# Column means of an 8192 x 8192 matrix: the mid-stream loads move to GpSimd's queue, eight descriptors to a packet

## The chip, the cores and the metric

The kernel runs on one core of a Trainium2 chip. A core has five engines with an instruction stream each: TensorE (PE, matmuls), VectorE (DVE, elementwise work on 128 partitions), ScalarE (ACT), GpSimd (POOL) and SyncE (SP, which here only issues transfers and waits). Data comes from the device's memory into the on-chip memory SBUF through 16 DMA engines, which work through queues of descriptors. A descriptor names one contiguous piece to be moved. TensorE writes its sums to a memory of its own, PSUM.

The metric is the device time of one execution in microseconds (us). The profile gives the span of one profiled execution, which is a little shorter than the time.

## The reference

```python
def setup_inputs():
    return {"x": np.random.randn(8192, 8192).astype(np.float32)}

def reference(x):
    return np.mean(x, axis=0)
```

The input has 268.4 MB, the output 32 KB. Each element is read once and added once. What is computed is a sum over 8192 rows for each of 8192 columns, divided by 8192.

## The kernel before

The 8192 rows are 64 groups of 128 rows, one row for each partition. VectorE adds group after group into an accumulator `acc` of 128 x 8192. Then TensorE sums over the 128 partitions: a matmul with a matrix `ones` whose elements are 1/8192. The last groups go to TensorE without passing VectorE.

SBUF holds six row buffers of 32 KB per partition each. Four of them, in two pairs, receive loads; the fifth (`both`) takes the sum of a pair; the sixth is `acc`.

```python
bufs = sb.tile([P, U, N], f32, name="bufs")      # P = 128, U = 6, N = 8192
both = bufs[:, U - 2, :]
acc = bufs[:, U - 1, :]
...
def load(dst, src):                              # every load comes from SyncE
    ins = tc.keep_in_program_order(nc.sync.dma_start(out=dst, in_=src)).ins
    ...
def load_rows(g, u, n):                          # n row groups; a partition gets n adjacent rows
    return load(bufs[:, u:u + n, :], rows(g, n).rearrange("(p j) c -> p j c", j=n))
```

With n = 2 each partition gets two adjacent rows, 64 KB that are contiguous in the device's memory and in SBUF.

The stream begins with part of a late row group (`head`), four row groups at once, two row groups, and part of the last row group (`ahead`):

```python
headed = load(head[:], rows(G - 4)[:, :3 * F])                # 768 KB, F = 512, G = 64
first, second = load_rows(0, 0, 4), load_rows(4, 4, 2)        # 16 MB, 8 MB
early = load(ahead[:], rows(G - 1)[:, 8 * F:WHOLE * F])       # 1 MB, WHOLE = 12
add(bufs[:, 2:4, :], bufs[:, 2:4, :], bufs[:, 0:2, :], [first])
add(bufs[:, 4:6, :], bufs[:, 4:6, :], bufs[:, 2:4, :], [second])
add(acc, acc, both, [])
```

Mid-stream has 24 rounds. Each loads two row groups and adds them:

```python
while g < G - 10:                                 # g = 6, 8, ..., 52
    u = (g + 2) % 4
    dma = load_rows(g, u, 2)
    add(both, bufs[:, u, :], bufs[:, u + 1, :], [dma])   # frees the pair of buffers
    add(acc, acc, both, [])
    if g == 20:
        add(acc[:, 8 * F:WHOLE * F], acc[:, 8 * F:WHOLE * F], ahead[:], [early])
    if g == 28:
        add(acc[:, :3 * F], acc[:, :3 * F], head[:], [headed])
    g += 2
```

`add` is a VectorE addition. Where it needs a transfer and the add ahead of it, a no-op on ScalarE (or now and then GpSimd) waits for both and releases the addition.

The end: six single row groups, two cut ones, group 62 (loaded whole) and group 63 in pieces. The last piece, columns 7168 to 8191, is loaded as two blocks of 512 columns, and each block is summed by four matmuls of 128 columns, so that the first block can be summed while the second is still on its way.

```python
for lo, hi in [(0, 8), (12, 14), (14, 15), (15, 16)]:
    load(r63[:, lo * F:hi * F], rows(g)[:, lo * F:hi * F])
plan = [(acc, 3, 5), (acc, 0, 3), (r61, 0, 5), (acc, 5, 12), (r62, 0, 12), (r62, 12, 13),
        (acc, 12, 14), (acc, 14, 16), (r63, 0, 8), (r63, 12, 14), (r63, 14, 15), (r63, 15, 16)]
```

`plan` is the order of the matmuls on TensorE; numbers are blocks of 512 columns. ScalarE and VectorE then copy the sums from PSUM to SBUF, and four small stores write the result.

Of the kernel before, what the change touches and what calls it, by code (L numbers as in the profile page):

```python
# [9 lines left out]
def kernel(  # L10
# [27 lines left out]
    nc = tc.nc  # L38
    f32 = mybir.dt.float32
    M, N = x.shape  # L40
    P = nc.NUM_PARTITIONS
    F = 512
    W = F // 2
    WHOLE = 12
    G = M // P
# [3 lines left out]
    sb = ctx.enter_context(tc.tile_pool(name="sb", bufs=1))  # L49
    psp = ctx.enter_context(tc.tile_pool(name="psum", bufs=1, space=bass.MemoryType.PSUM))  # L50

    bufs = sb.tile([P, U, N], f32, name="bufs")
    both = bufs[:, U - 2, :]
    acc = bufs[:, U - 1, :]
    ones = sb.tile([P, 32], f32, name="ones")
    ahead = sb.tile([P, 4 * F], f32, name="ahead")
    tail = sb.tile([P, 2, F // 4], f32, name="tail")
    warm = sb.tile([P, 32], f32, name="warm")
    nc.gpsimd.memset(ones[:], 1.0 / M)  # L59
    ready = sb.tile([P, 1], f32, name="ready")  # L60
    tc.keep_in_program_order(
        nc.gpsimd.tensor_add(out=ready[:], in0=ones[:, 0:1], in1=ones[:, 1:2]))  # L62
    banks = [psp.tile([P, F], f32, name=f"bank{b}") for b in range(3)]
    ends = [psp.tile([P, W], f32, name="end0"), psp.tile([P, 2, F // 4], f32, name="end1")]

    loads = []

    def landed(*inss):

        nop = tc.keep_in_program_order(nc.sync.nop()).ins  # L70
        for o in inss:
            tc.add_manual_dep(nop, o.name, sync, reason="SyncE waits")

    def load(dst, src):
        ins = tc.keep_in_program_order(nc.sync.dma_start(out=dst, in_=src)).ins
        k = len(loads)
        over = loads[k - 8:k - 6] if k >= 8 and k % 2 == 0 else []
        tc.declare_no_dep(ins, group="loads", keep=over, reason="the reader of the buffer waited")
        for o in over:
            tc.add_manual_dep(ins, o.name, sync, reason="covers the next load too")  # L80
        tc.add_to_no_dep_group("loads", ins)
        loads.append(ins)
        return ins

    def rows(g, n=1):
        return x[g * P:(g + n) * P, :]

    def load_rows(g, u, n):
        return load(bufs[:, u:u + n, :], rows(g, n).rearrange("(p j) c -> p j c", j=n))

    adds, joins = [], {}

    def add(dst, a, b, dmas):

        ins = nc.vector.tensor_add(out=dst, in0=a, in1=b).ins  # L95
        if dmas and adds:
            waiter = nc.scalar if len(adds) % 8 > 1 else nc.gpsimd
            nop = joins[waiter] = tc.keep_in_program_order(waiter.nop()).ins  # L98
            for o in dmas + adds[-1:]:
                tc.add_manual_dep(nop, o.name, sync, reason="the no-op waits")  # L100
            for group in ("loads", "adds"):
                tc.declare_no_dep(ins, group=group, reason="the no-op waited")
            tc.add_manual_dep(ins, nop.name, sync, reason="waits for both at once")
        elif adds:
            tc.declare_no_dep(ins, group="loads", reason="the add ahead waited")
        tc.add_to_no_dep_group("adds", ins)
        adds.append(ins)

    head = sb.tile([P, 3 * F], f32, name="head")
    headed = load(head[:], rows(G - 4)[:, :3 * F])  # L110
    first, second = load_rows(0, 0, 4), load_rows(4, 4, 2)
    early = load(ahead[:], rows(G - 1)[:, 8 * F:WHOLE * F])
    add(bufs[:, 2:4, :], bufs[:, 2:4, :], bufs[:, 0:2, :], [first])
    add(bufs[:, 4:6, :], bufs[:, 4:6, :], bufs[:, 2:4, :], [second])
    add(acc, acc, both, [])
    tc.keep_in_program_order(nc.scalar.copy(out=warm[:], in_=ones[:]))  # L116
    g = 6
    while g < G - 10:
        u = (g + 2) % 4
        dma = load_rows(g, u, 2)  # L120
        add(both, bufs[:, u, :], bufs[:, u + 1, :], [dma])
        add(acc, acc, both, [])
        if g == 20:
            add(acc[:, 8 * F:WHOLE * F], acc[:, 8 * F:WHOLE * F], ahead[:], [early])
        if g == 28:
            add(acc[:, :3 * F], acc[:, :3 * F], head[:], [headed])
        g += 2

    while g < G - 4:
        row = bufs[:, (g + 2) % 4, :]  # L130
        add(acc, acc, row, [load(row, rows(g))])
        g += 1
    for lo, loaded in [(3, 3), (5, 0)]:
        row = bufs[:, (g + 2) % 4, :]
        dma = load(row[:, loaded * F:], rows(g)[:, loaded * F:])
        add(acc[:, lo * F:], acc[:, lo * F:], row[:, lo * F:], [dma])
        g += 1
    r61, r62, r63 = [bufs[:, (g + 1 + j) % 4, :] for j in range(3)]
    load(r62, rows(g))
    tc.keep_in_program_order(nc.gpsimd.tensor_add(  # L140
        out=acc[:, 13 * F:], in0=acc[:, 13 * F:], in1=r62[:, 13 * F:]))
    g += 1
    for lo, hi in [(0, 8), (12, 14), (14, 15), (15, 16)]:
        load(r63[:, lo * F:hi * F], rows(g)[:, lo * F:hi * F])

    plan = [
        (acc, 3, 5),
        (acc, 0, 3),
        (r61, 0, 5),
        (acc, 5, 12),  # L150
        (r62, 0, 12),
        (r62, 12, 13),
# [1 line left out]
        (acc, 14, 16),  # L154
        (r63, 0, 8),
        (r63, 12, 14),
        (r63, 14, 15),
        (r63, 15, 16),
    ]
    sums = []  # L160
    for row, lo, hi in plan:
        if lo < WHOLE:
            for i in range(lo, hi):
                sums.append((banks[i // 4], i % 4, banks[i // 4], row[:, i * F:(i + 1) * F]))
        elif lo < 14:
            for c in range(lo * F, hi * F, W):
                e, q = divmod(c // W - 2 * WHOLE, 4)
                sums.append((ends[e], q, ends[e], row[:, c:c + W]))
        else:
            cols = row[:, 14 * F:].rearrange("p (b q c) -> p b q c", b=2, q=4)  # L170
            for q in range(4):
                b = slice(lo - 14, hi - 14)
                sums.append((ends[1], q, ends[1][:, b, :], cols[:, b, q, :]))
    for n, (dst, q, part, cols) in enumerate(sums):
        tc.keep_in_program_order(nc.tensor.matmul(  # L175
            out=part[32 * q:32 * q + 32],
            lhsT=ones[:],
            rhs=cols,
            start=all(d is not dst or k != q for d, k, _, _ in sums[:n]),
            stop=all(d is not dst or k != q for d, k, _, _ in sums[n + 1:]),  # L180
            tile_position=(0, 32 * q),
            skip_group_check=True,
        ))

    res = both[:, :3 * F].rearrange("p (b c) -> p b c", b=3)
    first_end = both[:, 3 * F:3 * F + W]

    def copy(dst, src):
        tc.keep_in_program_order(nc.scalar.copy(out=dst, in_=src))  # L189

    def store(engine, dst, src, *then):
        ins = tc.keep_in_program_order(engine.dma_start(out=dst, in_=src)).ins
        for o in then:
            tc.add_manual_dep(ins, o.name, sync, reason="follows that load")
        return ins

    copy(res[:, 2, :], banks[2][:])
    s2 = store(nc.scalar, out[8 * F:12 * F].rearrange("(q c) -> q c", q=4), res[0:P:32, 2, :],
               loads[-4])
    for b in range(2):  # L200
        copy(res[:, b, :], banks[b][:])
    copy(first_end, ends[0][:])
    nc.vector.tensor_copy(out=tail[:], in_=ends[1][:])  # L203
    landed(*loads[-8:-6])
    landed(*loads[-6:-4])
    landed(loads[-4])
    landed(*joins.values())
    s01 = store(nc.sync, out[:8 * F].rearrange("(b q c) -> q b c", b=2, q=4), res[0:P:32, 0:2, :])
    s3 = store(nc.scalar, out[12 * F:14 * F].rearrange("(q c) -> q c", q=4), first_end[0:P:32, :])
    store(nc.sync, out[14 * F:].rearrange("(b q c) -> q b c", b=2, q=4), tail[0:P:32, :, :])  # L210
    landed(loads[-3], s2)
    landed(loads[-2])
    landed(loads[-1], adds[-1])
    landed(s01, s3)
    hold = tc.keep_in_program_order(nc.vector.nop()).ins
# [31 lines left out]
```

## Time and profile before

| what | value |
|---|---|
| time, median of 3 | 629.1 us (629.0 to 629.31) |
| span of the profiled execution | 627.2 us |
| VectorE busy | 530.1 us (85%) |
| TensorE busy | 15.4 us (2%) |
| ScalarE, GpSimd busy | 3.5 us, 4.0 us |
| one addition of 128 x 8192 on VectorE | 8.69 us, 55 of them |
| one issue of a load on SyncE (median) | 0.33 us |
| one 8 MB load, issue to landing (median of its kind) | 29.9 us |

The page of the profile has parts: busy time by engine; the span in 40 equal slices, each with a digit for the busy share in tenths; the DMA queues with packets, bytes and the time that packets took; the chain of work that ended last, followed back from the end; groups of instructions with their mean duration and the idle time before them. A line such as `L95 DVE TENSOR_TENSOR` means line 95 of the kernel, VectorE, an addition of two tensors. `POOLq` and `ACTq` are instructions of these engines' queues that don't count as work, such as the no-ops. An engine's idle time costs something only if that engine is what the end waits for.

### The profile page before, as it was taken

Reading aid. Unit: us, or ns where it says so; the run is one execution under the profiler, and the core shown is the slowest. Engines: PE = TensorE matmul, PEld = TensorE weight load, DVE = VectorE, ACT = ScalarE, POOL = GpSimd, SP = SyncE. Lnnn points to the kernel's source line nnn. Section 1 sums busy time; section 2 is a strip of 40 time slices with the busy share of each in tenths; the row PEclk is TensorE's granted clock in tenths of the full one; section 3 lists DMA queues with packets and bytes.
Section 4 is the critical chain, followed back from the end, with each engine's and each line's share of the span. In section 5 each row is a group of like instructions: output and inputs, shape, how many; then the busy total and the mean of one; then the engine's idle time right before and its main releaser. Section 6 shows DMA issues by size and latency. Waiting matters only on the chain.

```text
span 627.2 us, 468 instructions
## 1 busy us (share of the span) xinstructions
PE 15.4 (2%) x118; PEld 4.9 (1%) x118; DVE 530.1 (85%) x62; ACT 3.5 (1%) x6; POOL 4.0 (1%) x7
## 2 busy tenths in 40 slices
PE   0000000000000000000000000000000000000027
PEld 0000000000000000000000000000000000000002
DVE  0028999999888999988998889888898888999991
ACT  0000000000000000000000000000000000000001
POOL 0000000000000000000000000000000000000002
PEclk9999999999999999999999999999999999999999
DMA  9999999999999999999999999999999999999996
GB/s 385 468 401 415 455 468 401 460 410 451 418 447 422 426 443 422 447 410 460 405 464 401 468 401 468 401 468 401 468 402 464 405 464 403 428 430 430 433 435 273
DMA packets 6074, 268.50 MB, mean 428 GB/s; under 512 B 672, under 2 KB 684, under 8 KB 1208
## 3 DMA queue, kind: packets, MB, share of 16 engines
q1 hardware_dynamic: 6056, 268.46, 99.1%
q8 instruction: 1, 0.02, 0.0%
q10 hardware_dynamic: 16, 0.01, 0.0%
q14 instruction: 1, 0.01, 0.0%
HBM read 268.44 MB, written 0.03 MB: 428 GB/s over the span
## 4 chain that ended last, share of the span: by engine, by line
DMA 55%; DVE 33%; another core or an unknown queue 10%; PE 0%; issue 0%; ACTq 0%; POOL 0%; POOLq 0%
DMA bufs<-in_x_dram 55%; DVE bufs L95 33%; PE bank L175 0%; PE end L175 0%; ACTq L98 0%; DVE tail L203 0%; POOLq L98 0%; POOL ready L62 0%; POOL ones L59 0%; POOLq L231 0%
## 5 line engine op out<-in xcount | busy, mean ns | idle before, releaser
L95 DVE TENSOR_TENSOR bufs<-bufs 128x8192 f32<-128x8192 f32 (+3 forms) x59 | 525.6, 8909 | 84.3 <-DMA bufs<-in_x_dram 43.7
L175 PE MATMUL bank<-bufs,ones 128*32 128x512 f32 x74 | 12.7, 713 | 608.7 <-DVE bufs L95 608.2
L203 DVE COPY tail<-end 128x256 f32<-128x256 f32 x1 | 0.4, 424 | 10.1 <-PE end L175 10.1
L175 PEld LDWEIGHTS bank<-bufs,ones 128*32 128x32 f32 x74 | 3.1, 120 | 616.9 <-issue 616.2
L140 POOL TENSOR_TENSOR bufs<-bufs 128x1536 f32<-128x1536 f32 x1 | 3.5, 3463 | 615.3 <-DMA bufs<-in_x_dram 615.3
L189 ACT COPY bufs<-bank 128x512 f32<-128x512 f32 x3 | 1.8, 585 | 619.8 <-PE bank L175 617.2
L175 PE MATMUL end<-bufs,ones 128*32 128x256 f32 (+1 forms) x44 | 3.2, 345 | 0.0
L95 DVE TENSOR_TENSOR bufs<-bufs,ahead 128x2048 f32<-128x2048 f32 x1 | 2.3, 2291 | 0.1
L95 DVE TENSOR_TENSOR bufs<-bufs,head 128x1536 f32<-128x1536 f32 x1 | 1.8, 1759 | 0.1
L175 PEld LDWEIGHTS end<-bufs,ones 128*32 128x32 f32 x44 | 1.8, 109 | 2.1 <-issue 0.8
L116 ACT ACT_TABLE_LOAD x1 | 1.3, 1283 | 0.7 <-PEq L231 0.7
L189 ACT COPY bufs<-end 128x256 f32<-128x256 f32 x1 | 0.4, 378 | 0.0
L116 ACT COPY warm<-ones 128x32 f32<-128x32 f32 x1 | 0.2, 218 | 0.0
L62 POOL TENSOR_TENSOR ready<-ones 128x1 f32<-128x1 f32 x1 | 0.2, 193 | 0.1
L59 POOL MEMSET ones<- 128x32 f32 x1 | 0.1, 124 | 0.3 <-POOLq L231 0.3
L231 POOL MEMSET const-bfloat16-1.0<- 128x1 bf16 x1 | 0.1, 101 | 0.0
L231 POOL MEMSET const-uint8-127<- 128x1 uint8 x1 | 0.1, 101 | 0.0
L231 POOL MEMSET const-float32-0.0<- 128x1 f32 x1 | 0.1, 98 | 0.2 <-issue 0.2
L231 POOL MEMSET const-float32-1.0<- 128x1 f32 x1 | 0.1, 98 | 0.0
## 6 DMA issues: line engine op xcount, KB each, us to landing
bufs<-in_x_dram SPq DMA_DIRECT2D x8, 4096.0 KB, 26.4
bufs<-in_x_dram SPq DMA_DIRECT2D x1, 3328.0 KB
bufs<-in_x_dram SPq DMA_DIRECT2D x1, 2048.0 KB, 20.3
ahead<-in_x_dram SPq DMA_DIRECT2D x1, 1024.0 KB
head<-in_x_dram SPq DMA_DIRECT2D x1, 768.0 KB
bufs<-in_x_dram SPq DMA_DIRECT2D x1, 512.0 KB, 21.1
bufs<-in_x_dram SPq DMA_DIRECT2D x2, 256.0 KB, 21.4
bufs<-in_x_dram SPq DMA_DIRECT2D x26, 29.9
```

Of the source, the lines that this page charges most:

```text
L59: nc.gpsimd.memset(ones[:], 1.0 / M)
L62: nc.gpsimd.tensor_add(out=ready[:], in0=ones[:, 0:1], in1=ones[:, 1:2]))
L95: ins = nc.vector.tensor_add(out=dst, in0=a, in1=b).ins
L116: tc.keep_in_program_order(nc.scalar.copy(out=warm[:], in_=ones[:]))
L140: tc.keep_in_program_order(nc.gpsimd.tensor_add(out=acc[:, 13 * F:], in0=acc[:, 13 * F:], in1=r62[:, 13 * F:]))
L175: tc.keep_in_program_order(nc.tensor.matmul(out=part[32 * q:32 * q + 32], lhsT=ones[:], rhs=cols, start=all(d is not dst or k != q for d, ...
L189: tc.keep_in_program_order(nc.scalar.copy(out=dst, in_=src))
L203: nc.vector.tensor_copy(out=tail[:], in_=ends[1][:])
L231: nc = _bacc.Bacc("TRN2", target_bir_lowering=False, num_devices=1)
```

## The change

The 24 mid-stream loads are issued by GpSimd in place of SyncE, with `single_packet=True`. In such a load each of the 16 DMA engines moves eight descriptors of 64 KB, and these form one packet. It is for a smaller cost of packets in the long middle of the stream.

Around it other parts differ. The no-ops all run on ScalarE, since GpSimd's stream now stands at its own loads. `ahead` and `head` are no longer added by VectorE in mid-stream; TensorE sums them at the end. The last piece of group 63 is one load of 1024 columns, summed by four matmuls of 256 columns.

```diff
+    def load_soft(dst, src):
+        ins = tc.keep_in_program_order(
+            nc.gpsimd.dma_start(out=dst, in_=src, single_packet=True)).ins
+        k = len(soft)
+        over = soft[k - 8:k - 7] if k >= 8 else []
+        ...
+        return ins
...
-            waiter = nc.scalar if len(adds) % 8 > 1 else nc.gpsimd
+            waiter = nc.scalar
...
-        dma = load_rows(g, u, 2)
+        dma = load_rows(g, u, 2, load_soft)
         add(both, bufs[:, u, :], bufs[:, u + 1, :], [dma])
         add(acc, acc, both, [])
-        if g == 20:
-            add(acc[:, 8 * F:WHOLE * F], acc[:, 8 * F:WHOLE * F], ahead[:], [early])
-        if g == 28:
-            add(acc[:, :3 * F], acc[:, :3 * F], head[:], [headed])
...
-    for lo, hi in [(0, 8), (12, 14), (14, 15), (15, 16)]:
+    for lo, hi in [(0, 8), (12, 14), (14, 16)]:
         load(r63[:, lo * F:hi * F], rows(g)[:, lo * F:hi * F])
...
     plan = [
+        (ahead, 8, 12),
         (acc, 3, 5),
         (acc, 0, 3),
         (r61, 0, 5),
+        (head, 0, 3),
         (acc, 5, 12),
...
-        (r63, 14, 15),
-        (r63, 15, 16),
+        (r63, 14, 16),
```

The rest of the diff (cut) follows from this: PSUM tiles and stores of the last piece have the plain order of columns, and the waits before the end name one load fewer.

More of the change, by code (lines that the diff above doesn't have):

```diff
@@ L56 @@
     ahead = sb.tile([P, 4 * F], f32, name="ahead")
-    tail = sb.tile([P, 2, F // 4], f32, name="tail")
+    tail = sb.tile([P, W], f32, name="tail")
     warm = sb.tile([P, 32], f32, name="warm")
@@ L63 @@
     banks = [psp.tile([P, F], f32, name=f"bank{b}") for b in range(3)]
-    ends = [psp.tile([P, W], f32, name="end0"), psp.tile([P, 2, F // 4], f32, name="end1")]
+    ends = [psp.tile([P, W], f32, name=f"end{e}") for e in range(2)]
     loads = []
@@ L72, in landed @@
             tc.add_manual_dep(nop, o.name, sync, reason="SyncE waits")
+    soft = []
+    def load_soft(dst, src):
[3 more added lines that the diff above has]
+        over = soft[k - 8:k - 7] if k >= 8 else []
+        tc.declare_no_dep(ins, group="loads", keep=over, reason="the reader of the buffer waited")
+        tc.add_to_no_dep_group("loads", ins)
+        soft.append(ins)
+        return ins
     def load(dst, src):
@@ L86, in rows, with load_rows @@
         return x[g * P:(g + n) * P, :]
-    def load_rows(g, u, n):
-        return load(bufs[:, u:u + n, :], rows(g, n).rearrange("(p j) c -> p j c", j=n))
+    def load_rows(g, u, n, how=load):
+        return how(bufs[:, u:u + n, :], rows(g, n).rearrange("(p j) c -> p j c", j=n))
     adds, joins = [], {}
@@ L109 @@
     head = sb.tile([P, 3 * F], f32, name="head")
-    headed = load(head[:], rows(G - 4)[:, :3 * F])
+    load(head[:], rows(G - 4)[:, :3 * F])
     first, second = load_rows(0, 0, 4), load_rows(4, 4, 2)
-    early = load(ahead[:], rows(G - 1)[:, 8 * F:WHOLE * F])
+    load(ahead[:], rows(G - 1)[:, 8 * F:WHOLE * F])
     add(bufs[:, 2:4, :], bufs[:, 2:4, :], bufs[:, 0:2, :], [first])
@@ L161 @@
     for row, lo, hi in plan:
+        base = 8 * F if row is ahead else 0
         if lo < WHOLE:
             for i in range(lo, hi):
-                sums.append((banks[i // 4], i % 4, banks[i // 4], row[:, i * F:(i + 1) * F]))
-        elif lo < 14:
+                cols = row[:, i * F - base:(i + 1) * F - base]
+                sums.append((banks[i // 4], i % 4, cols))
+        else:
             for c in range(lo * F, hi * F, W):
                 e, q = divmod(c // W - 2 * WHOLE, 4)
[L168 to L174, printed above, removed]
+                sums.append((ends[e], q, row[:, c:c + W]))
+    for n, (dst, q, cols) in enumerate(sums):
         tc.keep_in_program_order(nc.tensor.matmul(
-            out=part[32 * q:32 * q + 32],
+            out=dst[32 * q:32 * q + 32, :],
             lhsT=ones[:],
             rhs=cols,
-            start=all(d is not dst or k != q for d, k, _, _ in sums[:n]),
-            stop=all(d is not dst or k != q for d, k, _, _ in sums[n + 1:]),
+            start=all(d is not dst or k != q for d, k, _ in sums[:n]),
+            stop=all(d is not dst or k != q for d, k, _ in sums[n + 1:]),
             tile_position=(0, 32 * q),
@@ L185 @@
     res = both[:, :3 * F].rearrange("p (b c) -> p b c", b=3)
-    first_end = both[:, 3 * F:3 * F + W]
+    tails = [both[:, 3 * F:3 * F + W], tail[:]]
     def copy(dst, src):
@@ L195, in store, with end @@
         return ins
+    def end(e):
+        return (out[(WHOLE + 2 * e) * F:(WHOLE + 2 * e + 2) * F].rearrange("(q c) -> q c", q=4),
+                tails[e][0:P:32, :])
     copy(res[:, 2, :], banks[2][:])
     s2 = store(nc.scalar, out[8 * F:12 * F].rearrange("(q c) -> q c", q=4), res[0:P:32, 2, :],
-               loads[-4])
+               loads[-3])
     for b in range(2):
         copy(res[:, b, :], banks[b][:])
-    copy(first_end, ends[0][:])
-    nc.vector.tensor_copy(out=tail[:], in_=ends[1][:])
+    copy(tails[0], ends[0][:])
+    nc.vector.tensor_copy(out=tails[1], in_=ends[1][:])
     landed(*loads[-8:-6])
     landed(*loads[-6:-4])
-    landed(loads[-4])
+    landed(*loads[-4:-2])
     landed(*joins.values())
     s01 = store(nc.sync, out[:8 * F].rearrange("(b q c) -> q b c", b=2, q=4), res[0:P:32, 0:2, :])
[L209 to L212, printed above, removed]
+    s3 = store(nc.scalar, *end(0))
+    store(nc.sync, *end(1))
+    landed(loads[-2], s2)
     landed(loads[-1], adds[-1])
```

## The prediction

> **What bounds the kernel now.** I read the page first, then the chain of waits in order of time, then who waits for whom, and the groups by shape for the end. From the page, the rows of the 40 slices, the queue and the traffic:
>
> ```profile
> DVE  0028999999888999988998889888898888999991
> DMA  9999999999999999999999999999999999999996
> ...
> q1 hardware_dynamic: 6056, 268.46, 99.1%
> ...
> HBM read 268.44 MB, written 0.03 MB: 428 GB/s over the span
> ```
>
> The DMA row has a 9 in every slice but the last: the 16 DMA engines are busy from start to end, while VectorE is at 8 or 9 and has holes. All loads lie on one queue, 6056 packets, and their packets took 99.1% of 16 engines' span. 0.991 x 627.2 = 621.6 us, so only 5.6 us of the span are not transfer (about 2 us before the first packet, about 3.5 us after the last). The neighbouring slices that alternate between 401 and 468 GB/s are packets booked to one slice or the next; I read means of long stretches alone.
>
> The chain of waits (start, length, what), a piece of mid-stream:
>
> ```profile
> 190.35 29.93 DMA bufs<-in_x_dram
> 220.28 0.04 POOLq L98
> 220.31 0.02 issue
> 220.34 8.70 DVE bufs L95
> 229.04 0.02 issue
> 229.06 29.92 DMA bufs<-in_x_dram
> ```
>
> A load is issued when the first add of a pair frees its buffers, and lands 29.93 us later. From 190.35 to 229.06 are 38.71 us, and in this time two loads of 8 MiB pass (two pairs of buffers, so the chain hops over every second load): 16.78 MB / 38.71 us = 433.4 GB/s, 19.36 us a load. So of the 29.93 us, 29.93 - 19.36 = 10.6 us are queueing behind the load before. This is the margin by which an issue may be late in mid-stream before a DMA engine runs dry.
>
> At the start the margin is smaller:
>
> ```profile
> 63.10 17.24 DVE bufs L95
> 80.33 0.02 issue
> 80.36 8.70 DVE bufs L95
> 89.06 0.02 issue
> 89.08 0.05 ACTq L98
> 89.13 0.02 issue
> 89.15 8.70 DVE bufs L95
> 97.85 0.02 issue
> ```
>
> The second load of the program has landed at 63.0. Behind it lies the 1 MiB of "ahead" (1.05 MB / 433.4 = 2.4 us), to 65.4. The first of the 24 mid-stream loads is issued at 60.95 (the timeline shows SyncE issuing there): 4.4 us of margin. It ends at 65.4 + 19.36 = 84.8; the second is issued at 80.33: again 4.4. The third is issued at 97.85, when the one before it ends at 104.1: 6.3. VectorE then catches up and the margin grows to 10.6.
>
> The end, from the waits in total and the groups by shape:
>
> ```profile
> DVE bufs L95 <- ACTq L98: 25.2, 13, 2.6
> DVE bufs L95 <- POOLq L98: 13.2, 7, 2.2
> ...
> L175 PE MATMUL end<-bufs,ones 128*32 128x256 f32 x28 | 2.7, 382 | 0.0
> L175 PE MATMUL end<-bufs,ones 128*32 128x128 f32 x16 | 0.8, 279 | 0.0
> ```
>
> The no-ops named there only hand on a landing: VectorE waits 25.2 + 13.2 = 38.4 us in 20 places for loads. It isn't the bound. What remains is how fast the DMA engines go through their packets, and the few us after the last landing (PE's last matmuls, one copy of 0.42 us, one store).
>
> **What the Trainium skill says.** (1) "DMA: Bandwidth & Descriptors", section "Where 436 GB/s comes from": 16 ports x 32 B x 850 MHz = 435.2 GB/s is the ceiling, 27.2 GB/s an engine. The trace agrees from below: 433.4 in mid-stream. So at most 0.4% is to be had while bytes stay the same. (2) The same page, "Why small descriptors are slow (HBM only)": a fixed overhead of some 3 cycles for each packet inside the engine, which joining descriptors in one packet spreads out; it holds this worthwhile only up to 256 B. The trace shows a constant per descriptor of that kind: its single records of 64 KiB last 2421 ns on average and those of 32 KiB 1217 ns, and twice 1217 less 2421 is 13 ns. By the pace of mid-stream it is 19.36 us / 8 = 2419 ns a descriptor against 65536 B / 27.2 = 2409 ns: 10 ns. How much of this belongs to the packet rather than to the descriptor, no run here shows. (3) The same page, "Queues, rings and completion order": an engine goes round robin between its queues, a whole packet at a time. The kernel before has a single load queue, so its trace is silent. (4) "SBUF — State Buffer", section "Who interferes with whom": a VectorE instruction with two SBUF inputs contends with GpSimd's reads of SBUF only, and GpSimd's writing of descriptors is inferred to go on beside it. Before, GpSimd issues no load, so the trace is silent here too.
>
> **The change part by part.**
>
> 1. *24 loads as one packet of eight.* There are 24 x 8 = 192 descriptors of 64 KiB per engine in these loads, 24 x 19.36 = 464.6 us of the stream. If the whole 10 ns belongs to the packet, seven of eight are saved: 24 x 7 x 10 ns = 1.7 us. If only 3 cycles do, at the 850 MHz of the ceiling, it is 24 x 7 x 3.5 ns = 0.6 us. I take the middle: -1.2 us. As every load's add waits for its landing and the stream never pauses, each ns saved per load moves all that follows, so this counts in full.
>
> 2. *GpSimd issues in place of SyncE.* SyncE's issue takes 0.33 us by the trace; what one by GpSimd takes no run here shows. Up to 4.4 us (the smallest margin; then 6.3, and up to 10.6) it is hidden. I choose to believe that it is: 0.
>
> 3. *Two queues at the seams.* At the first seam the 8 MiB packet group arrives after 60.95, when the second load has about one descriptor per engine left (its last starts 2.4 us before 63.0) and the 1 MiB of "ahead" waits behind. "ahead" may now come later by one soft packet, 19 us; nothing needs it before the end, since its add is gone from VectorE. At the second seam the row loads from SyncE arrive while the last packet group runs, and with one packet per engine they can't cut in: 0.
>
> 4. *VectorE loses two adds* (2.29 + 1.76 = 4.05 us). They lay in mid-stream, where it waits 1.9 us a load: 0. All no-ops move to ScalarE, the same 0.03 to 0.05 us each: 0.
>
> 5. *PE gains seven matmuls.* Four on "ahead" run early. Three on "head" come between the row-61 matmuls and the wait for the last add, while PE is still slow: 34 records take 7.95 us there, 0.23 each, so 6 records 1.4 us. PE then starts the last acc columns at about 615, and row 62 up to 0.5 us later than now. The GpSimd add that ends at 619.86 gates PE anyway, so I count 0 to 0.1 us.
>
> 6. *Last piece whole.* One load of 512 KB, eight descriptors of 4 KiB per engine, in place of sixteen of 2 KiB: -8 x 10 ns = -0.08 us. After its landing PE has four matmuls of 256 columns (eight records, mean 382 ns, overlapped) in place of four of 128 (279 ns): +0.1 to 0.2. Together with part 5: +0.1 us.
>
> Sum: 629.1 - 1.2 + 0.1 = 628.0 us.
>
> **The rivals.**
>
> *The constant belongs to the descriptor, not to the packet.* Then part 1 gives nothing, and 629.1 + 0.1 = 629.2 results. For it: tiny records of 4 B in the trace also last 9 ns, so a descriptor costs something in whatever packet. Against: the wording of the skill. I give it a third.
>
> *Descriptors can't be written while VectorE adds.* An add starts 0.02 us after every issue, and lasts 8.7. The second mid-stream load would then be late by 8.7 - 4.4 = 4.3 us, the third a little more, and later ones stay within 10.6. The engines would show holes near 85 and 105 us, and the time would be 633 to 636. Against: the skill's inference. I give it 6%.
>
> *The soft ring is slower.* Its descriptors must be fetched from somewhere; 10 ns more per descriptor cost 192 x 10 ns = 1.9 us: 631. A first issue that takes over 4.4 us would add a hole of a few us once. 12%.
>
> *A big packet cuts ahead at the first seam.* If the first packet group starts on an engine before the second load's last descriptors, that load lands up to 19 us late, VectorE is late for all that follows, and the time goes towards 640. For: nothing orders two queues. Against: at 60.95 all but about one descriptor per engine are done. 2%.
>
> **Range and chances.** The best case is the ceiling for the 24 loads, 629.1 - 1.9 - 0.2 = 627.0; the common bad case is the slower ring or a late first issue, 630.5. These hold about eight in ten: 626.9 to 630.5. Faster by over 2% would be under 616.5 us, where 268.44 MB / 435.2 alone are 616.8: 1% for what I don't understand. Slower by over 2% is over 641.7 us, which only the cutting packet or holes in every load reach: 3%.
>
> **What would show it.** In the profile after: a second queue with 201 MB; the step between two landings at 19.27 to 19.30 us in place of 19.36 (part 1 right), or 19.36 (constant per descriptor), or more (slower ring); 9s in the DMA row from 60 to 110 us (no holes, parts 2 and 3); VectorE's second add of the double buffers still starting at 63.1; VectorE busy 526 us; PE's last matmuls ending within 0.2 us of where they stand against the last landing. The prediction is wrong if issues by GpSimd take over 4 us, or if the two queues share the engines in a way that delays a landing on which an add waits.

## The result, and the profile after

The changed kernel takes 631.44 us (631.28 to 631.52), the kernel before 629.05 us beside it. The ratio is 1.0037, with a 95% interval of 1.002 to 1.0054: the change costs 2.4 us. It was predicted to gain 1.1, and the range ended at 630.5.

The page of the changed kernel: 40 slices, queues and traffic.

```profile
DVE  0028999998888998888988889888889886999992
...
DMA  9999999999999999999999999999999999999995
...
q0 software_dynamic: 3456, 201.33, 73.9%
q1 hardware_dynamic: 2452, 67.13, 24.8%
...
HBM read 268.44 MB, written 0.03 MB: 426 GB/s over the span
```

The DMA row has no hole. The two queues' packets took 73.9% + 24.8% of 629.6 us, 621.4 us, where the one queue took 621.6 us before: nothing was saved, and nothing was lost either. What is new stands in VectorE's row: a 6 in slice 34 (about 519 to 535 us) where all its neighbours have 8 or 9.

The chain of waits of the changed kernel shows the pace of mid-stream, and then what became of the end. Columns are start, length, what.

```profile
191.20 0.52 POOL bufs L78
191.73 18.80 issue
...
210.54 0.52 POOL bufs L78
...
500.82 33.31 DMA bufs<-in_x_dram
534.12 0.03 ACTq L110
534.16 0.02 issue
534.18 8.70 DVE bufs L107
...
604.46 7.10 DVE bufs L107
611.56 0.04 issue
611.61 6.09 PE bank L181 x24
617.70 0.04 issue
617.73 3.86 PE bank L181 x33
...
625.04 1.10 PE end L181 x11
626.13 0.02 issue
626.16 0.42 DVE tail L213
```

From one issue to the next are 210.54 - 191.20 = 19.34 us; before it was half of 38.71, 19.36. Over the 15 loads from 191.20 to 481.48 it is 19.35 us, and over the 12 loads from 190.35 to 422.56 of the kernel before 19.35 too. So mid-stream keeps its pace. The last of GpSimd's loads (row groups 52 and 53) is issued at 500.82 and lands after 33.31 us, not 29.9. VectorE's timeline (start, length, instructions, idle time before), first of the kernel before, then of the changed one:

```profile
530.66 83.51 DVE L95 TENSOR_TENSOR bufs<-bufs 128x8192 f32<-128x8192 f32 x10 [1.93 <-ACTq L98]
```

```profile
534.18 83.50 DVE L107 TENSOR_TENSOR bufs<-bufs 128x8192 f32<-128x8192 f32 x10 [5.57 <-ACTq L110]
```

The wait for the last pair is 5.57 us in place of 1.93, 3.64 more. From there VectorE runs its last ten additions without a pause, as it did before, and everything it hands to TensorE comes 3.5 us later. Before, the chain waited for a transfer near its end:

```profile
600.88 20.26 DMA bufs<-in_x_dram
```

It ended at 621.14. Now from 611.6 on the chain is TensorE's matmuls, and those from 617.73 on had waited 0.94 us for VectorE's last addition (until 617.68). VectorE's last copy starts at 626.16 in place of 624.24.

Who held up the last of GpSimd's loads is seen by asking for the DMA queues in the 8 us from 523 to 531 alone (packets, MB, share of 16 engines), in the changed kernel:

```profile
q0 software_dynamic: 32, 2.10, 60.6%
q1 hardware_dynamic: 32, 1.05, 30.4%
```

Two descriptors of 64 KB and two of 32 KB per engine went in turn. SyncE had issued its first row loads at 519.91, when the buffers of the pair before came free. The records of single transfers come, from 524.4 us on, in groups of sixteen, one for each engine: 32, 64, 32, 64, 32 KB, and then the 4-byte record that signals the load's completion. These sixteen last records lie at 532.9 to 533.7 us; in a kernel with one queue for everything (mid_from_sync_5 below) they lie at 528.9 to 529.3, straight behind the data. Three foreign records of 1.217 us are 3.65 us, and VectorE's wait has grown by 3.64.

So the theory, called "seam": where GpSimd's queue hands over to SyncE's, the DMA engines serve both queues descriptor by descriptor. The row loads get their bytes early, when VectorE has no time for them, and the last pair gets its bytes late, when VectorE waits for it. At this place no record lasts longer than elsewhere (2.42 and 1.22 us). The rivals were "tail" (the sums on TensorE and the whole last piece cost the time) and "GpSimd" (its loads are slower or are issued too late).

### The profile page after: what moved, and what is told of

It reads as the page before. It is cut to its first block, busy times and chain, and to the rows that moved or that the text cites. A ratio compares the mean times of both kernels' runs of the same rounds, so it can differ in the third digit from the quotient of the medians.

```text
span 629.6 us, 482 instructions
## 1 busy us (share of the span) xinstructions
PE 16.4 (3%) x124; PEld 4.9 (1%) x124; DVE 526.1 (84%) x60; ACT 3.5 (1%) x6; POOL 16.8 (3%) x31
## 3 DMA queue, kind: packets, MB, share of 16 engines
q0 software_dynamic: 3456, 201.33, 73.9%
q1 hardware_dynamic: 2452, 67.13, 24.8%
## 4 chain that ended last, share of the span: by engine, by line
issue 51%; DVE 25%; DMA 10%; another core or an unknown queue 10%; PE 2%; POOL 1%; ACTq 0%; POOLq 0%
DVE bufs L107 25%; DMA bufs<-in_x_dram 10%; PE bank L181 2%; POOL bufs L78 1%; PE end L181 0%; ACTq L110 0%; DVE tail L213 0%; POOLq L78 0%; POOLq L148 0%
## 5 line engine op out<-in xcount | busy, mean ns | idle before, releaser
L78 POOL DMA_DIRECT2D bufs<-in_x_dram x24 | 12.8, 535 | 487.4 <-DVE bufs L107 487.4
L181 PE MATMUL end<-bufs,ones 128*32 128x256 f32 x36 | 4.1, 381 | 0.0
L181 PE MATMUL bank<-ahead,ones 128*32 128x512 f32 x8 | 1.9, 1058 | 65.6 <-DMA ahead<-in_x_dram 65.6
L181 PE MATMUL bank<-head,ones 128*32 128x512 f32 x6 | 1.9, 600 | 0.0
L181 PEld LDWEIGHTS bank<-ahead,ones 128*32 128x32 f32 x8 | 0.2, 140 | 65.6 <-issue 65.6
```

Source lines behind the costliest of these rows:

```text
L78: nc.gpsimd.dma_start(out=dst, in_=src, single_packet=True)).ins
L181: tc.keep_in_program_order(nc.tensor.matmul(out=dst[32 * q:32 * q + 32, :], lhsT=ones[:], rhs=cols, start=all(d is not dst or k != q for d ...
```

## The experiments

All but two are edits of the changed kernel.

**mid_from_sync: one queue again**

```diff
-        dma = load_rows(g, u, 2, load_soft)
+        dma = load_rows(g, u, 2)
```

> The changed kernel with its 24 mid-stream loads issued by SyncE again; the sums of head and ahead on TensorE, the whole last piece and the no-ops on ScalarE stay. Theory 'seam' (the last load of GpSimd's queue lands 3.6 us late because SyncE's row loads share the DMA engines with it): there is one queue, so VectorE's add on the last pair starts near 530.6 us, not 534.2, and the time is 629.1, at most 0.3 off. Rival 'tail' (the extra matmuls and the whole last piece cost the 2.4 us): it stays at 631.2 to 631.6. Rival 'GpSimd' (its loads are slower or issued too late): 629.1 as well, so this run speaks only against 'tail'.

Measured: 628.74 us (628.45 to 628.98), ratio to the kernel before 0.9994 (0.9985 to 1.0003), 0.1 us under the expected range. VectorE's timeline at the last pair:

```profile
530.16 83.50 DVE L107 TENSOR_TENSOR bufs<-bufs 128x8192 f32<-128x8192 f32 x10 [1.95 <-ACTq L110]
```

The wait is the usual one again. "Tail" falls: the loss goes with the queue.

**act_queue: the same seam between two hardware queues**

```diff
-            nc.gpsimd.dma_start(out=dst, in_=src, single_packet=True)).ins
+            nc.scalar.dma_start(out=dst, in_=src)).ins
...
-            waiter = nc.scalar
+            waiter = nc.gpsimd
```

> The changed kernel with the 24 mid-stream loads issued by ScalarE (a hardware queue, no single packet) and the no-ops moved to GpSimd, so that a second queue hands over to SyncE's row loads at the same place without any load of GpSimd. 'Seam': the row loads of 32 KB descriptors again come between the last 64 KB descriptors, the last pair lands about 3.6 us late (add at 534 us), time 631.0 to 631.8. 'GpSimd': 629.1, as nothing of GpSimd is left. 'Tail': 631.4, but with the last pair landing at 530.6.

Measured: 630.70 us (630.47 to 630.86), ratio 1.0025 (1.0015 to 1.0036); 0.3 us under the expected range. VectorE's waits in total and at longest (us in total, times, longest), and the queues from 523 to 531:

```profile
DVE bufs L107 <- POOLq L110: 45.8, 22, 5.6
```

```profile
q10 hardware_dynamic: 32, 2.10, 60.6%
q1 hardware_dynamic: 32, 1.05, 30.4%
```

The same 5.6 us wait for the last pair (others in mid-stream are 1.9), the same split of the 8 us. Most of the loss needs no load of GpSimd's, only a second queue. Against mid_from_sync (628.74, measured beside it) the seam costs 2.0 us. This kernel stands 1.6 us above the kernel before, the changed one 2.4: the other 0.8 us goes with GpSimd's loads.

**gate: SyncE's row loads wait 8.7 us longer**

```diff
+        if g == G - 10:
+            tc.add_manual_dep(dma, adds[-3].name, sync, ...)   # the accumulator's addition
```

> The changed kernel, with one more wait: SyncE's first row load waits for the accumulator's addition that ends about 8.7 us later (528.6 us in place of 519.9), when the last GpSimd load has about one descriptor per engine left. 'Seam': the last pair lands at 530.6 to 531.8, the row loads follow with a hole of at most 1 us, time 629.0 to 630.2. 'GpSimd' and 'tail': 631.4 or more, as nothing else changed and the row loads start later.

Measured: 630.01 us (629.71 to 631.37), ratio 1.0017 (1.001 to 1.0023). The last pair is in time, at 530.42, and the end of the chain waits for a transfer again:

```profile
600.60 0.02 issue
...
601.47 22.80 DMA bufs<-in_x_dram
624.27 0.04 issue
624.31 0.68 PE end L184 x8
624.99 0.02 issue
625.02 0.42 DVE tail L216
```

So starting the row loads later makes the kernel faster by 1.4 us than the changed one, which the rivals exclude. It isn't free: the last copy starts at 625.02, 1.4 us later than in mid_from_sync_5 (623.64). Part of it is the handover itself: the first 32 KB record on each engine, behind the last of GpSimd's, lasts 1.3 to 2.2 us in place of 1.217. The gate trades a wrong order for a slow start of SyncE's loads.

**all_pool: GpSimd issues all later loads too**

```diff
-        add(acc, acc, row, [load(row, rows(g))])
+        add(acc, acc, row, [load_late(row, rows(g))])     # load_soft; likewise all loads behind it
```

> The changed kernel with all later loads (six row groups, two cut ones, group 62 and the pieces of group 63) issued by GpSimd as well, its own addition behind them: there is no second seam, and more loads are GpSimd's. 'Seam': the last pair lands at 530.6 and the time is 628.9 to 629.8. 'GpSimd': 631.4 or more, with more loads of the slow kind at the end. 'Tail': 631.4.

Measured: 629.16 us (628.87 to 629.56), ratio 1.0001 (0.9992 to 1.0009); the last pair at 530.64. With 12 more loads of GpSimd's and no seam the loss is gone but for some 0.5 us against mid_from_sync_5. "GpSimd" falls as the main cause; the 0.5 us that stay are taken up below.

**no_single: without the packet flag**

```diff
-            nc.gpsimd.dma_start(out=dst, in_=src, single_packet=True)).ins
+            nc.gpsimd.dma_start(out=dst, in_=src)).ins
```

> The changed kernel without single_packet. 'Seam' with descriptors as the unit of switching (what the records of the changed kernel show: 32 KB and 64 KB descriptors in turn): nothing changes, the last pair lands at 534 us, time 631.2 to 631.6, and the 64 KB records last 2.42 us as before. If the packet does hold descriptors together in part, the last pair lands later than 534 us and the time rises, or the mean 64 KB record grows by up to 10 ns (1.7 us in all).

Measured: 631.30 us (631.1 to 631.82), ratio 1.0033 (1.002 to 1.0046). Again from 523 to 531:

```profile
q0 software_dynamic: 32, 2.10, 60.6%
q1 hardware_dynamic: 32, 1.05, 30.4%
```

The same time, the same turn-taking, and 64 KB records of 2422 ns on average with and without the flag (2421 in the kernel before). For these loads the flag does nothing that a run shows: it neither saves a cost between descriptors nor keeps another queue out. That the eight descriptors form one packet, as the section on the change has it, no run shows: the records name descriptors. So it stays open whether the engines switch inside a packet or each of these descriptors is a packet of its own.

**seam_early: the seam four rounds before**

```diff
-        dma = load_rows(g, u, 2, load_soft)
+        dma = load_rows(g, u, 2, load_soft if g < 46 else load)
```

> The changed kernel with the last four mid-stream loads (row groups 46 to 53) issued by SyncE, so that the seam lies four rounds earlier, where a load of 64 KB descriptors comes between. 'Seam': the load at the seam lands about 3 x 2.42 = 7.3 us late, but VectorE idles 1.9 us in each round of 19.36 us and the load behind lands early, so that the delay is made good before the end; the last pair's add starts within 1 us of 530.6 us, time 629.0 to 629.9. A theory in which any seam costs what it costs in the changed kernel says 631.4 or, as the delay is doubled, 633 to 635.

Measured: 628.92 us (628.65 to 630.36), ratio 0.9998 (0.999 to 1.0007), 0.1 us under the expected range. The page, and VectorE's timeline from 470 us on (start, length, instructions, idle time before):

```profile
DVE  0028999998888998888988889888769999999991
```

```profile
477.54 52.46 DVE L107 TENSOR_TENSOR bufs<-bufs 128x8192 f32<-128x8192 f32 x6
530.19 83.50 DVE L107 TENSOR_TENSOR bufs<-bufs 128x8192 f32<-128x8192 f32 x10 [0.19 <-ACTq L110]
```

The hole is in slices 29 and 30 now: VectorE waits 9.2 us for the load at the seam (its addition starts at 460.02), 7.3 more than usual, three records of 2.42. Behind it VectorE works through three rounds without the usual 1.9 us waits, as the loads that came between are there early. At 530.19 it is even. A late landing with idle time behind it costs nothing; the changed kernel has its seam just ahead of the stretch in which VectorE has none.

**pair_at_seam: the double dose**

```diff
-    while g < G - 10:
+    while g < G - 8:
-        dma = load_rows(g, u, 2, load_soft)
+        dma = load_rows(g, u, 2, load_soft if g < G - 10 else load)
```

> The changed kernel with row groups 54 and 55 as one SyncE load of 64 KB descriptors in place of two of 32 KB, so that what comes between the last GpSimd descriptors is twice as long. 'Seam': the last pair lands about 3 x 2.42 = 7.3 us late in place of 3.65 (add near 538 us), VectorE's last addition ends near 621.5 us in place of 617.7, time 634 to 636. If the lateness comes from GpSimd's completion or issue and not from what comes between, it stays 3.6 us and the time 631 to 632.

Measured: 635.02 us (634.8 to 635.33), ratio 1.0093 (1.0076 to 1.0109).

```profile
DVE bufs L107 <- ACTq L110: 49.9, 22, 9.2
```

The longest wait is 9.2 us in place of 5.6, VectorE starts on the last pair at 537.76 (534.18 in the changed kernel), and the time with it: 5.8 us above the kernel before in place of 2.4. What comes between sets the lateness, and once VectorE is the bound of the end, lateness counts nearly in full. The first 3.6 us cost only 2.0 to 2.2 (act_queue against mid_from_sync and mid_from_sync_5): the rest was slack that TensorE and VectorE had against the last transfers.

**before_soft: the kernel before, with the queue alone changed**

```diff
+    def load_soft(dst, src): ...     # as in the changed kernel
...
-        dma = load_rows(g, u, 2)
+        dma = load_rows(g, u, 2, load_soft)
...
-            waiter = nc.scalar if len(adds) % 8 > 1 else nc.gpsimd
+            waiter = nc.scalar
```

> The kernel before with nothing changed but the queue: the 24 mid-stream loads come from GpSimd with single_packet, and the no-ops that GpSimd held go to ScalarE. Head and ahead are still added by VectorE, the last piece is still two loads. 'Seam': the last pair lands 3.6 us late (add near 534 us), time 631.0 to 631.8, the same as the changed kernel. If the other parts of the change add to its loss: 630.5 or less.

Measured: 632.24 us (632.0 to 632.42), ratio 1.0046 (1.0033 to 1.006), 0.4 us above the expected range. VectorE starts on the last pair at 534.91. The queue alone costs 3.0 us against the kernel before beside it (629.27), the whole change 2.4. So the other parts of the change gain some 0.6 us rather than cost any.

**before_pe_sums: the kernel before, with the sums on TensorE alone**

```diff
-            waiter = nc.scalar if len(adds) % 8 > 1 else nc.gpsimd
+            waiter = nc.scalar
...
-        if g == 20:
-            add(acc[:, 8 * F:WHOLE * F], ..., ahead[:], [early])
-        if g == 28:
-            add(acc[:, :3 * F], acc[:, :3 * F], head[:], [headed])
...
     plan = [
+        (ahead, 8, 12),
...
+        (head, 0, 3),
...
```

> The kernel before, all loads from SyncE and the last piece as two loads, with head and ahead summed by TensorE in place of VectorE and all no-ops on ScalarE. It tells what of the 0.4 us between the kernel before and mid_from_sync comes from the whole last piece. If the whole last piece is what gains, 629.0 to 629.2; if the sums on TensorE gain (two additions less in mid-stream), 628.6 to 628.9.

Measured: 628.39 us (628.16 to 629.0) beside 629.27, ratio 0.9987 (0.998 to 0.9993). It is faster than both kernels, and faster than expected. Part of the 0.9 us is in the trace. The queues from 455 to 475 us, in the kernel before:

```profile
q1 hardware_dynamic: 144, 8.39, 97.1%
q14 instruction: 1, 0.01, 0.1%
```

and in before_pe_sums:

```profile
q1 hardware_dynamic: 144, 8.39, 96.9%
```

In the kernel before, one fetch of 8 KB of instructions falls into the stream. One 64 KB record beside it lasts 3.08 us in place of 2.42, and the load it belongs to lands 0.66 to 0.7 us late (VectorE waits 2.64 us at 472.61, not 1.93). The engine stays behind: at the last pair the sixteen completion records spread over 1.2 us (528.9 to 530.1), in mid_from_sync_5 over 0.4. before_soft has the same fetch, and the same wait. The kernels with the sums on TensorE have none at this place. That the fetch costs this is read from these traces; no run changed it by itself. The rest, 0.2 us, isn't located.

**mid_from_sync_5: the same as mid_from_sync, in more rounds**

> mid_from_sync again in more rounds, beside the kernel before on one chip: whether the changed kernel without its second queue beats both kernels. 628.6 to 628.9 against 629.0 to 629.2, with an interval that leaves out 1, if the 0.4 us is real; 629.0 if it was chance.

Measured: 628.63 us (628.45 to 628.87) beside 629.27, ratio 0.999 (0.9984 to 0.9997). The changed kernel without its queue is faster than both, too, and 0.24 us slower than before_pe_sums, which differs in the last piece.

## Why the prediction was wrong

The bound of mid-stream was read rightly: the DMA engines are busy all through. What the prediction left out is that VectorE ("It isn't the bound") had little slack at the end, some 1.5 us: of a lateness of 3.6 us about 2.1 count. The sum, step by step, from the kernel before through before_pe_sums, mid_from_sync_5 and act_queue to the changed kernel (each taken as its distance from the kernel before measured beside it, which took 629.05 to 629.27; rounded steps):

| step | predicted | measured |
|---|---|---|
| parts 4 and 5, sums on TensorE | 0 to +0.1 | -0.9 |
| part 6, last piece whole | 0 to +0.1 | +0.2 |
| part 3, seam between two queues | 0 | +2.2 (+2.0 against mid_from_sync) |
| parts 1 and 2, GpSimd and its packets | -1.2 | +0.8 |

*Part 3 is the step that failed.* It said of the second seam that the row loads of SyncE "arrive while the last packet group runs, and with one packet per engine they can't cut in". They cut in after every descriptor, the last pair landed 3.6 us late, and the 0 was 2.0 to 2.2 us. I took from the Trainium skill ("DMA: Bandwidth & Descriptors", "Queues, rings and completion order") that an engine changes queue only between packets, and from the flag's name that eight descriptors are one packet. The turn-taking is there, as that page says; its unit in these traces is the descriptor, flag or not. The rival of a cut-in was named, but for the first seam and at 2%; the second seam was where it mattered. Among its signs of being wrong the prediction also named that the two queues delay a landing on which an add waits, and gave this no cost. I had the number that shows why it matters: in the kernel before, VectorE starts its last ten additions at 530.66 and doesn't wait again, so a late landing there has no idle time behind it, while in mid-stream 1.9 us are free in each round. That the rival of a slower ring said 631, close to the 631.4 measured, is chance: its 10 ns more per descriptor would show in mid-stream, and there the 64 KB records last 2422 ns, against 2421 before.

*Part 1* had its sign from one choice: that most of the 10 ns per 64 KB descriptor belong to the packet. Nothing of it went (2421 ns a record before, 2422 after). The rival "the constant belongs to the descriptor", at a third, was right in its result.

*Part 2* was right that GpSimd's issue (0.53 us, 0.70 the first time) is hidden, and VectorE's additions don't hold it up, in agreement with the skill ("SBUF — State Buffer", "Who interferes with whom"). Even so GpSimd costs. VectorE starts on the last pair but two at 491.83, in act_queue at 491.19 and in mid_from_sync_5 at 491.18; of these 0.6 us, 0.1 lies ahead of the first addition. Part of the rest is in the records: the first 64 KB record of GpSimd's first load lasts up to 2.88 us on an engine (2.85 to 3.24 at most in all seven kernels with GpSimd's loads), and with ScalarE's queue at the same place 2.418 us on all sixteen. This comes from the traces alone; no run took it away by itself.

*The first seam* did as predicted in effect, but not in kind: "ahead" wasn't pushed behind a packet. It landed at 65.6, where TensorE begins its matmuls.

*Part 4* expected nothing from two additions less where VectorE waits anyway. That holds for VectorE; the gain comes, by the traces, for the most part from an instruction fetch that no longer falls among the loads.

*Part 6* estimated 0.1 for both ends together; the whole last piece costs 0.24 us (628.39 and 628.63, medians of 21 executions each).

## What to carry to other kernels

Loads that must land in order belong in one queue: in these runs, with descriptors of 32 and 64 KB, a second queue that started early took its share descriptor by descriptor from the load that was waited for, though the DMA engines lost nothing. If a handover can't be avoided, put it where the waiting engine has idle time behind it, or hold the second queue back until the last load is nearly through. Before one believes that a flag joins descriptors, compare the records of single transfers with and without it.

## What was not expected of the hardware

The signal of completion takes its turn too: the 4-byte record of the last pair came behind a third foreign descriptor, 1.217 us after the data were through. By the traces, a single fetch of 8 KB of instructions cost a stream at full load about 0.7 us: one DMA engine fell behind (a record of 3.08 us in place of 2.42), and was still behind at the last pair, and a load has landed only when its slowest engine is through.
